# Neighbourhood attention: each head's probabilities divided on GpSimd before they are transposed

## The chip, the cores and the metric

The kernel runs on one core of a Trainium2 chip. The metric is the device time of one execution in microseconds, median of several runs. The core has a matrix engine (TensorE, PE in rows), VectorE (DVE), ScalarE (ACT), GpSimd (POOL) and SyncE (SP), which here only issues DMAs. Each engine works through its own instructions in program order, so an instruction that waits holds up everything behind it on that engine.

## What is computed

One step of a two-layer backbone over 128 context tokens and 2048 latent tokens (a grid of 32 rows by 64 columns), model width 1024. In a layer an input projection feeds four mixers of width 256 each, their gated outputs are joined and go through an output projection and a layer normalisation. The change touches mixer B, the neighbourhood attention of the latent tokens, with 4 heads of 64:

```
s_loc = einsum(q, k of 8 rows x 16 columns around the query) * scale + bias
s_ctx = einsum(q, 256 context keys) * scale
p     = softmax(concat(s_loc, s_ctx))
o     = p_loc @ v_loc + p_ctx @ v_ctx
mixed = o * SiLU(gate)
```

## The kernel before

The time of a layer falls into four stages: input projection and convolution (`phase1`), grouped-query attention (`phase2`), neighbourhood attention (`phase3`), output projection with layer normalisation (`phase4`). The program is written in plain order and a scheduler at build time sets the order on every engine from its own estimate of times; on the chip that order is fixed. It orders TensorE freely in `phase3`.

`phase3` works on 16 tiles of a layer: 8 groups of four grid rows (`NAT_ORDER` = 1, 2, 0, 3, 4, 5, 7, 6), each in a left and a right half (e = 0, 1), so 128 queries a tile. A tile has four heads. Here the heads of a layer are counted through from 0 to 63 in the order of work: head 8 is the first of the third tile. A pair is two heads that share one call of `values`. Inner tiles have 440 local keys and 256 context keys (696 columns); the four tiles of groups 0 and 7 (heads 16 to 23 and 48 to 55, called edge tiles) have 576 columns. For each head:

- S (`scores`, L1222 and L1223): four matmuls into one of two `ps_d` banks.
- TTR (L1228, VectorE): adds the bias, writes `p` to SBUF and takes the row maximum; then m (L1231) negates it. `p` comes from a pool of three buffers (`b3`).
- E (L1232, ScalarE): exp in place, with the row sum into `z`.
- T (`transp`, L1255): five or six transpositions by matmul with the identity, in two parts; VectorE copies part 0 to SBUF (C, L1257), ScalarE part 1 (C', L1259).
- V (`values`, L1270): for a pair of heads, 24 (edge tiles 20) records of values times transposed probabilities into `ps_a`.

`finish` (L1275) ends a tile: reciprocal of the four sums (L1278), copy to a 128x256 tile `zb` (L1279), two matmuls with the identity that spread the reciprocals into the other half of the `ps_a` bank (Z, L1281), and four VectorE products with the gate (L1290): first gate by reciprocal, then by the sums of values.

Two things beside that run in the stage. `load_p4pre` (called at step 8) prepares the output projection's weights: four loads `wo` through two buffers, each cast by ScalarE (woh, L1409) and then subtracted by GpSimd (wol, L1410); the third load needs the buffer that the first wol frees. And `prompt_attn` does the context tokens' attention twice (L1361 to L1391). The first blocks of `phase4` (L1452: `mx`, `mhi`, `mlo`) are prepared late in the stage, and its matmuls (L1492 to L1494) begin while the last heads are still at work.

Of the kernel before, what the change touches and what calls it, by code (L numbers as in the profile page):

```python
# [8 lines left out]
F32 = mybir.dt.float32  # L9
F32R = mybir.dt.float32r  # L10
AF = mybir.ActivationFunctionType
ALU = mybir.AluOpType
# [108 lines left out]
class Kern:  # L121
# [1047 lines left out]
    def _phase3(self, l):  # L1169
        nc, A, S = self.nc, self.A, self.S  # L1170
# [20 lines left out]
        def begin(i, e):  # L1191
            x = tiles.index((i, e))
            if e == 0:
                x = x // 2
                if x + 2 < NT:
                    self.load_nq(NAT_ORDER[x + 2])
                gates[i] = self.b2.tile([128, 2, 256], F32, tag="gt", name="gt")
                c0 = NPR + i * 256
                nc.sync.dma_start(gates[i], S["gate"][256:512, c0:c0 + 256].rearrange("(c p) t -> p c t", p=128))
            d = {"bias": held["tile", i] if d_edge(i) else bi, "v": self.nv[e]}  # L1200
            d["q"] = [
                t[:, :, e * 128:(e + 1) * 128] for t in self.nq[i]
            ]
            d["z"] = self.b2.tile([128, 4], F32, tag="z", name="z")
            st[i, e] = d

        def d_edge(i):
# [2 lines left out]
        def scores(i, e, h):  # L1210
            d = st[i, e]
            k0, nr = self.rows_of(i)
            q = d["q"]
            s = self.bank("d", (128, 1024))
# [3 lines left out]
            n = nr * KC  # L1218
# [5 lines left out]
            p = self.b3.tile([128, NLOC + PAST], F32, tag="p", name="p")  # L1224
            m = self.b3.tile([128, 2], F32, tag="m", name="m")
            n = nr * KC + PAST
# [2 lines left out]
                p[:, :n], s[:, o:o + n], d["bias"][:, h, b0:b0 + n], 1.0, -3.0e38, ALU.add, ALU.max, m[:, 0:1]  # L1229
            )  # L1230
            nc.vector.tensor_scalar(m[:, 1:2], m[:, 0:1], -1.0, None, op0=ALU.mult)  # L1231
            nc.scalar.activation(p[:, :n], p[:, :n], AF.Exp, bias=m[:, 1:2], accum_out=d["z"][:, h:h + 1])  # L1232
            d["p", h] = p

        def chunks(i, e):
# [26 lines left out]
        def values(i, e, pr):  # L1262
            d = st[i, e]
            if pr == 0:
                d["acc"] = self.bank("a", (128, 4, 128))
            ch = chunks(i, e)
            for c, (_, vt, ti) in enumerate(ch):
                for hh in range(2):
                    h = pr * 2 + hh
                    nc.tensor.matmul(  # L1270
                        d["acc"][hh * 64:(hh + 1) * 64, pr, :], vt[:, ti, h * 64:(h + 1) * 64], d["pT", h][:, c, :],
                        start=(c == 0), stop=(c == len(ch) - 1),
                    )

        def finish(i, e):  # L1275
            d = st.pop((i, e))
            zb = self.b2.tile([128, 4, 64], F32, tag="zb", name="zb", bufs=1)
            nc.vector.reciprocal(d["z"], d["z"])  # L1278
            nc.vector.tensor_copy(zb, d["z"].unsqueeze(2).to_broadcast([128, 4, 64]))  # L1279
            for c in range(2):  # L1280
                nc.tensor.matmul(  # L1281
                    d["acc"][:, 2 + c, :], zb[:, 2 * c:2 * c + 2, :].rearrange("p h d -> p (h d)"), self.id,
                    start=True, stop=True,
                )
            gt = gates[i]
            acc = d["acc"].rearrange("p a (r c) -> p a r c", r=4)
            for x in (1, 0):
                for c in range(2):
                    g = gt[:, c, :].rearrange("p (r s c) -> p r s c", r=4, s=2)[:, :, e, :]
                    nc.vector.tensor_tensor(g, acc[:, 2 * x + c], g, op=ALU.mult)  # L1290
            if e == 1:
                c0 = NPR + i * 256
                nc.sync.dma_start(S["mix"][256:512, c0:c0 + 256].rearrange("(c p) t -> p c t", p=128), gates.pop(i))

        pairs = [(i, e, pr) for i, e in tiles for pr in range(2)]
        n = len(pairs)
# [394 lines left out]
```

## Time and profile before

| | us |
|---|---|
| median of 3 runs | 2995.2 |
| lowest and highest of them | 2991.32, 3001.62 |
| the profiled execution's own time | 2991.36 |
| its span, first to last instruction | 2989.6 |
| TensorE busy in the span | 2783.8 (93%) |
| VectorE busy | 2070.4 (69%) |
| GpSimd busy | 1456.9 (49%) |
| ScalarE busy | 1272.3 (43%) |
| `phase3` of layer 0, first S to the first output-projection matmul | 1156.0 to 1315.8 |
| the same in layer 1 | 2630.1 to 2787.4 |

Busy shares of the whole span mix stages with different limits; what counts for this change is what stands in the two stretches of the last two lines. A busy TensorE need not be at its peak, since matmuls overlap in the records.

### The profile page before, as it was taken

How to read it: one execution, taken by the hardware profiler on the slowest of the kernel's cores; microseconds unless marked ns; L12 is line 12 of the kernel's file. 1: busy time of each engine (PE TensorE's matmuls, PEld its weight loads, DVE VectorE, ACT ScalarE, POOL GpSimd, SP SyncE). 2: the span in 40 equal slices, each digit the busy share in tenths (PEclk: the TensorE clock that was granted, in tenths of full speed). 3: DMA queues.
4: the chain of work that ended last, by engine and by line, in shares of the span. 5: the costliest groups of instructions: out<-in, count | busy, mean ns of one | idle time of the engine just before them, and what ended most of it. 6: DMA issues, size and time to landing. Idle time of an engine off the chain costs nothing.

```text
span 2989.6 us, 47085 instructions
## 1 busy us (share of the span) xinstructions
PE 2783.8 (93%) x16944; PEld 2287.9 (77%) x16944; DVE 2070.4 (69%) x4119; ACT 1272.3 (43%) x2376; POOL 1456.9 (49%) x1170
## 2 busy tenths in 40 slices
PE   8888999899899999999989889988899999999998
PEld 6778988889755555887778889988896555578887
DVE  2595168974588886759855971699655788777587
ACT  4454433554344445542224544435533444465311
POOL 4666344654366666004325674456634666740232
PEclk9999999999999999999999999999999999999999
DMA  8343464454370104646642335523443610057342
GB/s 267 106 135 117 131 192 139 127 159 123 102 168 20 34 18 132 158 149 223 212 147 82 116 105 128 160 89 116 146 123 82 144 34 20 24 168 191 132 165 106
DMA packets 390569, 372.82 MB, mean 125 GB/s; under 512 B 52672, under 2 KB 370112, under 8 KB 388800
## 3 DMA queue, kind: packets, MB, share of 16 engines
q1 hardware_dynamic: 390336, 369.82, 42.5%
q8 instruction: 133, 2.18, 0.3%
q14 instruction: 100, 0.82, 0.1%
HBM read 254.66 MB, written 115.06 MB: 124 GB/s over the span
## 4 chain that ended last, share of the span: by engine, by line
PE 56%; DVE 23%; DMA 9%; POOL 4%; ACT 3%; issue 3%; SPq 2%; DVEq 0%; ACTq 0%; POOLq 0%
DVE cacc L755 8%; PE ps_a L1011 7%; PE ps_u L304 5%; PE ps_u L305 5%; PE ps_u L306 5%; PE ps_d L990 4%; PE ps_d L1000 4%; PE ps_d L1493 3%; PE ps_d L1492 3%; PE ps_d L1494 3%; PE ps_a L1270 3%; PE ps_s L928 3%; POOL cac L753 2%; PE ps_s L1255 1%; PE ps_z L928 1%
## 5 line engine op out<-in xcount | busy, mean ns | idle before, releaser
L304 PE MATMUL ps_u<-hhi,whi 128*128 128x384 f32 (+1 forms) x1728 | 576.2, 336 | 2.7 <-ACT hhi L387 2.7
L305 PE MATMUL ps_u<-hlo,whi 128*128 128x384 f32 (+1 forms) x1728 | 576.3, 334 | 1.3 <-DVE hlo L389 0.8
L306 PE MATMUL ps_u<-hhi,wlo 128*128 128x384 f32 (+1 forms) x1728 | 575.3, 333 | 0.0
L1023 POOL TENSOR_TENSOR zp<-zp,e 128x1024 f32<-128x1024 f32 x160 | 385.9, 2412 | 209.8 <-ACT e L1005 206.4
L1005 ACT ACTIVATE e<-ps_d 128x1024 f32<-128x1024 f32 x288 | 292.1, 1024 | 358.6 <-PE ps_d L1000 349.3
L755 DVE SCALAR_TENSOR_TENSOR cacc<-cz,small,cacc 128x208 f32<-128x208 f32 (+2 forms) x840 | 427.5, 565 | 0.3
L419 POOL TENSOR_TENSOR wlo<-ws,whi 128x512 fp32r<-128x512 f32 x188 | 261.1, 1401 | 198.8 <-ACT whi L418 182.8
L304 PEld LDWEIGHTS ps_u<-hhi,whi 128*128 128x128 f32 x1728 | 331.7, 193 | 10.8 <-ACT hhi L387 5.6
L305 PEld LDWEIGHTS ps_u<-hlo,whi 128*128 128x128 f32 x1728 | 332.5, 192 | 6.4 <-POOL hlo L389 2.4
L306 PEld LDWEIGHTS ps_u<-hhi,wlo 128*128 128x128 f32 x1728 | 332.1, 192 | 0.9
L1463 POOL TENSOR_TENSOR mlo<-mx,mhi 128x512 fp32r<-128x512 f32 x66 | 110.4, 1691 | 421.0 <-ACT mhi L1459 405.7
L931 DVE TENSOR_REDUCE mx<-ps_s 128x1 f32<-128x512 f32 (+1 forms) x374 | 228.5, 631 | 107.2 <-PE ps_s L928 102.6
L753 POOL TENSOR_TENSOR cac<-cac,ctm 128x208 f32<-128x208 f32 (+2 forms) x320 | 244.9, 765 | 104.8 <-ACT ctm L752 69.6
L1011 PE MATMUL ps_a<-e,gvv 128*64 128x512 f32 x1152 | 278.2, 604 | 0.0
L304 PE MATMUL ps_u<-whi,hhi 128*128 128x256 f32 x816 | 237.1, 291 | 4.0 <-ACT ev L543 4.0
L306 PE MATMUL ps_u<-whi,hlo 128*128 128x256 f32 x816 | 235.5, 289 | 0.0
L305 PE MATMUL ps_u<-wlo,hhi 128*128 128x256 f32 x816 | 235.5, 289 | 0.0
L752 ACT ACTIVATE ctm<-cz,small 128x208 f32<-128x208 f32 (+2 forms) x320 | 148.5, 472 | 149.7 <-POOL cac L753 91.7
L1493 PE MATMUL ps_d<-wol,mhi 128*128 128x512 f32 x512 | 201.0, 393 | 0.0
L1492 PE MATMUL ps_d<-woh,mhi 128*128 128x512 f32 x512 | 201.0, 393 | 0.0
L1494 PE MATMUL ps_d<-woh,mlo 128*128 128x512 f32 x512 | 200.1, 391 | 0.0
L1000 PE MATMUL ps_d<-q,k 65*128 65x512 f32 x576 | 185.6, 403 | 12.0 <-DMA k<-s_k 12.0
(269 smaller groups left out, 5834.0 us busy)
## 6 DMA issues: line engine op xcount, KB each, us to landing
ws<-in_w_in SPq DMA_DIRECT2D x160, 256.0 KB
mw<-in_w_mod SPq DMA_DIRECT2D x32, 512.0 KB
nq<-s_nq SPq DMA_DIRECT2D x64, 256.0 KB
mx<-s_mix SPq DMA_DIRECT2D x16, 1024.0 KB
s_gate<-ev SPq DMA_DIRECT2D x80, 192.0 KB
s_qh<-qT SPq DMA_DIRECT2D x34, 256.0 KB
x<-in_x SPq DMA_DIRECT2D x17, 512.0 KB
s_xT<-xo SPq DMA_DIRECT2D x17, 512.0 KB
```

Of the source, the lines that this page charges most:

```text
L304: mm(p, ah, bh, start=(k == 0), stop=False)
L305: mm(p, ah, bl, start=False, stop=False)
L306: return mm(p, al, bh, start=False, stop=(k == 7))
L753: nc.gpsimd.tensor_tensor(ac2[:, :n], ac2[:, :n], tm[:, :n], op=ALU.add)
L755: nc.vector.scalar_tensor_tensor(acc[:, c, :n], z[:, c, k:k + n], cw[:, c, k:k + 1], acc[:, c, :n], op0=ALU.mult, op1=ALU.add)
L1000: nc.tensor.matmul(s[:, kv * 512:(kv + 1) * 512], k2[kv][0:65, j * 128:(j + 1) * 128], q2[0:65, 2 * kv:2 * kv + 2, :].rearrange("p h t -> ...
L1005: nc.scalar.activation(e, s, AF.Exp)
L1011: nc.tensor.matmul(acc[kv * 64:(kv + 1) * 64, :], vv[:, j, kv * 64:(kv + 1) * 64], e[:, kv * 512:(kv + 1) * 512], start=(j == 0), stop=(j ...
L1023: nc.gpsimd.tensor_tensor(zp, zp, e, op=ALU.add)
L1492: nc.tensor.matmul(o, hi[:, k, :], woh[:, k, ns], start=(k == 0), stop=False)
L1493: nc.tensor.matmul(o, hi[:, k, :], wol[:, k, ns], start=False, stop=False)
L1494: nc.tensor.matmul(o, lo[:, k, :], woh[:, k, ns], start=False, stop=(k == 7))
```

## The change

Each head's sum now goes into the first column of its own `m`; VectorE takes its reciprocal (R, new L1232), GpSimd multiplies the head's probabilities by it in place (sc, new L1233, 128x696 or 128x576 f32), and the transpositions read the product. The tile `z`, the reciprocal and copy of `finish`, the two Z matmuls and two of the four gate products of a tile go. Lines behind L1204 shift by a few.

```diff
-            d["z"] = self.b2.tile([128, 4], F32, tag="z", name="z")
...
             nc.vector.tensor_scalar(m[:, 1:2], m[:, 0:1], -1.0, None, op0=ALU.mult)
-            nc.scalar.activation(p[:, :n], p[:, :n], AF.Exp, bias=m[:, 1:2], accum_out=d["z"][:, h:h + 1])
+            nc.scalar.activation(p[:, :n], p[:, :n], AF.Exp, bias=m[:, 1:2], accum_out=m[:, 0:1])
+            nc.vector.reciprocal(m[:, 0:1], m[:, 0:1])
+            nc.gpsimd.tensor_scalar(p[:, :n], p[:, :n], m[:, 0:1], None, op0=ALU.mult)
             d["p", h] = p
...
-                d["acc"] = self.bank("a", (128, 4, 128))
+                d["acc"] = self.bank("a", (128, 2, 128))
...
-            zb = self.b2.tile([128, 4, 64], F32, tag="zb", name="zb", bufs=1)
-            nc.vector.reciprocal(d["z"], d["z"])
-            nc.vector.tensor_copy(zb, d["z"].unsqueeze(2).to_broadcast([128, 4, 64]))
-            for c in range(2):
-                nc.tensor.matmul(
-                    d["acc"][:, 2 + c, :], zb[:, 2 * c:2 * c + 2, :].rearrange("p h d -> p (h d)"), self.id,
-                    start=True, stop=True,
-                )
             gt = gates[i]
             acc = d["acc"].rearrange("p a (r c) -> p a r c", r=4)
-            for x in (1, 0):
-                for c in range(2):
-                    g = gt[:, c, :].rearrange("p (r s c) -> p r s c", r=4, s=2)[:, :, e, :]
-                    nc.vector.tensor_tensor(g, acc[:, 2 * x + c], g, op=ALU.mult)
+            for c in range(2):
+                g = gt[:, c, :].rearrange("p (r s c) -> p r s c", r=4, s=2)[:, :, e, :]
+                nc.vector.tensor_tensor(g, acc[:, c], g, op=ALU.mult)
```

The scheduler sets the whole stage anew. On GpSimd, at the start of layer 0's stage, the order of the change is this (L1233 is sc, L1402 is wol, L1079 belongs to the stage before; before, GpSimd had only L1079 and the four wol here):

```order
382 L1233 TENSOR_SCALAR p<-p,m 128x696 [waits DVE_49]
383 L1079 TENSOR_TENSOR accs<-accs,zd 128x512 [waits DVE_49,Activation_49,Pool_49]
384 L1233 TENSOR_SCALAR p<-p,m 128x696 [waits DVE_49] x2
385 L1233 TENSOR_SCALAR p<-p,m 128x696 [waits DVE_49,PE_49] x2
386 L1402 TENSOR_TENSOR wol<-wo,woh 128x2048 [waits DMAHW5_49,Activation_49]
387 L1402 TENSOR_TENSOR wol<-wo,woh 128x2048 [waits DMAHW6_49,Activation_49]
388 L1233 TENSOR_SCALAR p<-p,m 128x696 [waits DVE_49,PE_49] x3
389 L1402 TENSOR_TENSOR wol<-wo,woh 128x2048 [waits DMAHW6_49,Activation_49]
390 L1402 TENSOR_TENSOR wol<-wo,woh 128x2048 [waits DMAHW7_49,Activation_49]
391 L1233 TENSOR_SCALAR p<-p,m 128x696 [waits DVE_49,PE_49] x8
```

So the products of heads 0 to 4 stand ahead of the first two wol, those of heads 5 to 7 between the two pairs, and head 8 behind the last; in layer 1 the order is the same.

On TensorE in the middle of the stage, this is the order of the change from the transpositions of head 34 on (L1256 is T, L1271 V, L1221 and L1222 S; the S is that of head 39, the V that of heads 34 and 35):

```order
5675 L1256 MATMUL ps_s<-small,p 128x128 [waits PE_49,Pool_49]
5676 L1256 MATMUL ps_s<-small,p 128x128 x2
5677 L1256 MATMUL ps_z<-small,p 128x128 [waits PE_49]
5678 L1256 MATMUL ps_z<-small,p 128x128 x2
5679 L1271 MATMUL ps_a<-pT,nv_9314 64x128 [waits DVE_49]
5680 L1256 MATMUL ps_s<-small,p 128x128 [waits PE_49,Pool_49]
5681 L1256 MATMUL ps_s<-small,p 128x128 x2
5682 L1256 MATMUL ps_s<-small,p 128x128 [waits PE_49]
5683 L1256 MATMUL ps_s<-small,p 128x128 x2
5684 L1221 MATMUL ps_d<-ck_9311,nq_12470 128x256 [waits DVE_49]
```

And this is the order of before from the transpositions of head 34 on (L1255 is T, L1270 V; this V is that of the pair before, heads 32 and 33):

```order
5653 L1255 MATMUL ps_s<-small,p 128x128 [waits Activation_49]
5654 L1255 MATMUL ps_s<-small,p 128x128 x2
5655 L1255 MATMUL ps_z<-small,p 128x128 [waits DVE_49]
5656 L1255 MATMUL ps_z<-small,p 128x128 x2
5657 L1270 MATMUL ps_a<-pT,nv_9314 64x128 [waits DMAHW1_49,DMAHW0_49,DMAHW2_49,DVE_49,PE_49]
5658 L1270 MATMUL ps_a<-pT,nv_9314 64x128 x6
5659 L1255 MATMUL ps_s<-small,p 128x128 [waits Activation_49]
5660 L1255 MATMUL ps_s<-small,p 128x128 x2
5661 L1270 MATMUL ps_a<-pT,nv_9314 64x128
5662 L1270 MATMUL ps_a<-pT,cvt 64x128 x4
```

Before, the V behind a pair's first T belongs to the pair before it; after, it is the pair's own V, one T behind. On VectorE this is the order of the change from the TTR of head 37 on (L1227 is TTR with its read of the maximum, L1230 m, L1232 R, L1258 C; the first C is that of head 35, the last that of head 36):

```order
1340 L1227 ISA p,m<-ps_d,bi 128x696 [waits PE_49,Pool_49]
1341 L1227 ISA m 128x1
1342 L1230 TENSOR_SCALAR m<-m 128x1 [waits DVE_49]
1343 L1258 COPY pT<-ps_s 128x384 [waits PE_49]
1344 L1227 ISA p,m<-ps_d,bi 128x696 [waits PE_49,Pool_49]
1345 L1227 ISA m 128x1
1346 L1232 RECIPROCAL m<-m 128x1 [waits Activation_49]
1347 L1230 TENSOR_SCALAR m<-m 128x1 [waits DVE_49]
1348 L1282 TENSOR_TENSOR gt<-ps_a,gt 128x4x32 [waits DMAHW3_49,DMAHW2_49,PE_49]
1349 L1282 TENSOR_TENSOR gt<-ps_a,gt 128x4x32
1350 L1232 RECIPROCAL m<-m 128x1 [waits Activation_49]
1351 L1258 COPY pT<-ps_z 128x384 [waits PE_49]
```

The copy of head 34 stands right ahead of the first of these rows, so the TTR of head 37 follows it; the same holds for head 36 and the TTR of head 39. The R of a pair's first head waits for the exp of the m just ahead of it. On ScalarE the order in a pair is E of head 36, C' of 34, E of 37, C' of 35, E of 38 and so on.

## Rows read from the trace of the kernel before

**Rows 1.** Windows: us, busy of PE, PEld, DVE, ACT, POOL, granted clock, DMA share, GB/s.

```profile
1157.00:1316.00 159.00, 152.25 (x1378) 127.85 (x1376) 118.04 (x360) 95.78 (x210) 24.67 (x9) 0.98 0.69 190
2631.00:2787.00 156.00, 150.60 (x1377) 125.18 (x1377) 116.98 (x359) 95.33 (x210) 25.21 (x9) 0.99 0.70 194
...
1276.00:1296.00 20.00, 17.69 (x157) 15.29 (x157) 12.28 (x42) 10.89 (x26) 1.28 (x1) 0.91 0.78 206
```

**Rows 2.** Groups by line, 1157 to 1316: shapes, count, busy, mean ns, idle before.

```profile
L1290 DVE TENSOR_TENSOR gt<-ps_a,gt 128x128 f32<-128x128 f32 x56 | 13.2, 282 | 1.4 <-PE ps_a L1281 1.0
...
L1281 PE MATMUL ps_a<-small,zb 128*128 128x128 f32 x56 | 10.2, 299 | 0.0
...
L1279 DVE COPY zb<-z 128x256 f32<-128x256 f32 x15 | 7.1, 474 | 0.0
...
L1371 ACT ACTIVATE pp<-ps_d,pm 128x128 f32<-128x128 f32 x8 | 2.8, 361 | 0.8 <-DVE pm L1367 0.8
...
L1278 DVE RECIPROCAL z<-z 128x4 f32<-128x4 f32 x15 | 2.6, 171 | 1.5 <-ACT p L1232 1.5
```

**Rows 3.** Groups by line and form on GpSimd, whole span.

```profile
L1410 POOL TENSOR_TENSOR wol<-wo,woh 128x2048 fp32r<-128x2048 f32 x8 | 36.7, 4609 | 25.9 <-ACT woh L1409 25.9
...
L1124 POOL MEMSET nv<- 128x1024 f32 x4 | 3.7, 958 | 0.0
```

**Rows 4.** Timeline of GpSimd, both layers: start, us, what, idle before.

```profile
1176.91 9.18 POOL L1410 TENSOR_TENSOR wol<-wo,woh 128x2048 fp32r<-128x2048 f32 x2 [8.80 <-ACT woh L1409]
1190.78 9.14 POOL L1410 TENSOR_TENSOR wol<-wo,woh 128x2048 fp32r<-128x2048 f32 x2 [4.70 <-ACT woh L1409]
...
2649.59 9.18 POOL L1410 TENSOR_TENSOR wol<-wo,woh 128x2048 fp32r<-128x2048 f32 x2 [8.49 <-ACT woh L1409]
2662.66 9.16 POOL L1410 TENSOR_TENSOR wol<-wo,woh 128x2048 fp32r<-128x2048 f32 x2 [3.88 <-ACT woh L1409]
```

**Rows 5.** Timeline of TensorE: T of head 8 (both layers), S, T and V.

```profile
1179.44 0.37 PE L1222 MATMUL ps_d<-nk,nq 128*128 128x440 f32 x1
...
1180.08 0.82 PE L1255 MATMUL ps_s<-small,p 128*128 128x128 f32 x6
...
1184.89 0.49 PE L1255 MATMUL ps_s<-small,p 128*128 128x128 f32 x3
...
1192.79 1.09 PE L1270 MATMUL ps_a<-pT,nv 128*64 128x128 f32 x16
...
1194.15 0.38 PE L1270 MATMUL ps_a<-pT,nv 128*64 128x128 f32 x2
...
2657.73 0.49 PE L1255 MATMUL ps_s<-small,p 128*128 128x128 f32 x3
```

**Rows 6.** Timeline of VectorE: a TTR, the C of head 8, a zb copy.

```profile
1160.35 0.87 DVE L1228 CUSTOM_DVE_ANT_0 p<-ps_d,bi 128x696 f32<-128x696 f32 x1
...
1185.49 0.56 DVE L1257 COPY pT<-ps_s 128x384 f32<-128x384 f32 x1 [0.61 <-PE ps_s L1255]
...
1192.66 2.84 DVE L1279 COPY zb<-z 128x256 f32<-128x256 f32 x1
```

**Rows 7.** Timeline of ScalarE: the E behind that TTR, another E, and its C'.

```profile
1161.45 0.88 ACT L1232 ACTIVATE p<-p,m 128x696 f32<-128x696 f32 x1 [2.91 <-DVE m L1231]
...
1170.23 0.86 ACT L1232 ACTIVATE p<-p,m 128x696 f32<-128x696 f32 x1
...
1171.09 0.47 ACT L1259 ACTIVATE pT<-ps_z 128x384 f32<-128x384 f32 x1
```

**Rows 8.** One line's instructions: the output projection's, first and last start, each layer.

```profile
L1492 PE MATMUL ps_d<-woh,mhi x256: 387/389/692, 1315.8 to 1521.2; 128*128 128x512 f32 x128
...
L1492 PE MATMUL ps_d<-woh,mhi x256: 387/389/476, 2787.4 to 2969.3; 128*128 128x512 f32 x128
```

**Rows 9.** Windows at layer 0's start of the stage, columns as in rows 1.

```profile
1164.00:1168.00 4.00, 1.79 (x13) 1.23 (x12) 4.00 (x12) 1.78 (x4) 1.17 (x1) 1.00 0.52 177
1168.00:1172.00 4.00, 4.00 (x30) 3.61 (x31) 3.16 (x11) 2.66 (x8) 0.10 (x1) 0.61 0.54 140
```

## The prediction

> **What bounds the kernel now.** The change lies wholly in `phase3`, so I read first the windows of that stage in both layers [rows 1]: TensorE is busy 152.25 of 159 us in layer 0 and 150.60 of 156 in layer 1, VectorE 118 and 117, ScalarE 96 and 95, GpSimd only 25. TensorE is the engine that ends last, GpSimd has room. Taken by shares, the change moves work from the full engine to the empty one. Then I read the groups by line for what goes [rows 2], the timelines around the four wol for what GpSimd does at the start of the stage [rows 4], and the single instructions of one head for the lengths of a chain [rows 5 to 7]. The reader should see in rows 4 that GpSimd's 25 us are not spread over the stage: they are four long subtractions, from 1176.91 to 1186.09 and from 1190.78 to 1199.92, and the same in layer 1. The new products go into that queue.
>
> **What is removed.** The Z matmuls were busy 10.2 us in 14 tiles of layer 0 [rows 2], 0.7 a tile, some 23 us in all 32 tiles if nothing else ended last. VectorE loses two gate products of 282 ns a tile, a zb copy (mean 474 ns) and one reciprocal (171 ns) [rows 2]. One of these copies took 2.84 us while wol was running [rows 6]; that goes too. VectorE gains a reciprocal and its wait for each head. The nearest row is the 171 ns of the 128x4 one [rows 2]; for 128x1 it can hardly be more and not be below nothing. It lies in a queue that is not the longest (below), so I charge no term.
>
> **What is added on GpSimd.** No row shows a multiply by a column. Above stands a subtraction with two inputs: wol takes 4609 ns for 2048 columns [rows 3], 2.25 ns a column, 1.57 us for 696. Below stands a fill with no input: 958 ns for 1024 [rows 3], 0.94 a column, 0.65 us. One tile input lies between; I take 1.0 us and keep 0.65 and 1.6. At 1.6 us a head GpSimd would still need only 3.2 us for a pair, so it is not the bound by its busy time.
>
> The Trainium skill (GPSIMD Engine Reference, 4.1 Engine selection) holds one-input elementwise work to be roughly at line rate and two-input work about twice slower than on VectorE. By that the multiply would sit near my lower end and take some 0.4 us off each layer; no run here shows it yet.
>
> **First term: the late start of head 8.** The four wol can't move forward. Each waits for a cast, each cast for a load, and the third load for the buffer that the first wol frees, so I take their times from before [rows 4]. The new order puts the products of heads 5 to 7 behind the second wol and that of head 8 behind the fourth. Head 8 is transposed no earlier than 1199.9 + 1.0 (product) + 0.1 (handover) = 1201.0. Before, its T began at 1184.89 [rows 5]: 16.1 us late. In layer 1, 2671.8 + 1.1 = 2672.9 against 2657.73 [rows 4, 5]: 15.2 us late. TensorE can't fill this with other heads, since `p` has three buffers and each is held until its own T. What it can do meanwhile is one V (below).
>
> **Second term: the pace after that.** Before, T of head 8 to the first output-projection matmul took 1315.8 - 1184.89 = 130.9 us, and 2787.4 - 2657.73 = 129.7 in layer 1 [rows 5, 8], prompts and stalls included. After, TensorE's work for an inner pair is two S of 0.64 (1179.44 to 1180.08), twelve T at 0.75 per six, 24 V in 1.36 (1192.79 to 1194.15) [rows 5]: 4.1 us. But the new order puts V right behind its own T, and so one chain goes once round per pair: half of V (0.68), S (0.64), T part 0 to the start of its C (1184.89 to 1185.49, 0.60), C 0.56 [rows 5, 6], then on VectorE the next TTR to its E (1160.35 to 1161.45, 1.10) [rows 6, 7], E to the C' behind it (1170.23 to 1171.09, 0.86), C' 0.47 [rows 7], handover 0.1, and the second half of V again. Sum 5.0 us. VectorE's own chain round a pair (two TTR, two C, one exposed E) is two TTR of 0.9, two C of 0.5 to 0.56, an E of 1.05 with m and R around it, some 4.4 us, and stays below. The multiply is not in the 5.0: each T reads a product begun a good third of a pair earlier or more. For edge tiles I scale by columns, 5.0 x 576/696 = 4.15, an estimate. From T of head 8 to the first output matmul stand 18 inner and 8 edge pairs: 90 + 33 = 123. The prompt blocks sit in the same queues with eight exps of 361 ns and their reads [rows 2]: 5. The wait for the first mix block cost TensorE 2.3 us idle and 9% of clock in 20 us [rows 1]: 4, and stays. One V of 1.4 was done during the late start, and the first pair behind it has looser order: -2. Sum 130. So this term is -0.9 in layer 0 and +0.3 in layer 1: the Z matmuls and the old stalls pay for the chain.
>
> **Third term: the end.** The first output matmul now stands behind V of heads 58 and 59; before, that V (1.4 us) and two tiles' Z (1.4) came behind it, and part of one T (0.35) before it. -2.4 us a layer.
>
> **Fourth term: the clock.** When TensorE was busy 1.79 of 4 us, the next 4 us stood at a granted clock of 0.61, a mix of its two levels of 1.2 and 2.4 GHz [rows 9]; that cost about 1.6 us. The late start leaves TensorE as idle, so I add 1.5 a layer.
>
> Layer 0: 16.1 - 0.9 - 2.4 + 1.5 = 14.3. Layer 1: 15.2 + 0.3 - 2.4 + 1.5 = 14.6. Together 29 us on the profiled execution's 2991.4: 3020. That execution lies 3.8 below the median of the runs shown, so a median may stand up to 4 higher; I say 3021.
>
> **The rivals.** First, *no change*: the late start comes as above, but the chain doesn't bind, because handovers overlap, and the pairs behind head 8 go at TensorE's work, 4.1 inner and 3.8 edge. Then the second term is 18 x 4.1 + 8 x 3.8 + 5 + 4 - 2 = 111, 19 below; with 15.7 late, -2.4 and +1.5 a layer ends 4 us earlier: 2983; with three quarters of that gain it ends level, 2992. For it speaks that before TensorE ran without a gap through most of the stage; against it the order, which leaves no other matmul between T and its V.
>
> Second, *faster*: the products are hidden and all of Z comes back, 2991 - 23 = 2968. It takes that head 8 is not late, so that wol ends 15 us sooner or the pairs make it up and more. Rows 4 speak against it: GpSimd waits there for casts and loads, which this change doesn't touch.
>
> Third, *much slower*: VectorE and GpSimd hinder each other. The zb copy of 2.84 us, six times its mean, ran inside the second stretch of wol [rows 4, 6]. If each C waited so for a product of 1.0 us, half of it on the chain, 26 pairs would lose 1 us each, 52 in both layers: 3073. Against it: the C at 1185.49 took 0.56 us inside the first stretch of wol [rows 4, 6]. C reads PSUM, zb's copy read SBUF.
>
> The Trainium skill (SBUF — State Buffer, Who interferes with whom) has this as a rule: a VectorE copy in a two-port mode and a GpSimd instruction lock each other out for a whole instruction, a VectorE instruction with at most one SBUF input outside those modes does not. Both rows agree with it; by it the remaining TTR, C and gate products would run freely, and the third rival falls.
>
> **How the numbers follow.** Forecast 0.70: 3021. With the multiply at its ends, the chain 0.2 us off per pair (5 us a layer) and the clock between 0 and 3 us a layer its own range is 3005 to 3040. Rival one 0.12 (2983 to 3000), rival two 0.05, rival three or a chain slowed further by low clock 0.13 (3040 to 3075). About 0.3% (9 us) is what a measurement here can tell from no change, so 2986 to 3004 is the same. Slower takes the forecast but 0.02, and rival three: 0.81. Same takes that 0.02 and 0.08 of rival one: 0.10. Faster: 0.09. A range from 2996 to 3048 leaves out about 2 in 10.
>
> **What would show it.** In the new profile: products of some 0.65 to 1.6 us on GpSimd, with gaps of more than 9 us between those of heads 4 and 5 and of heads 7 and 8, filled by wol at nearly the old times; T of head 8 about 15 us later than before, counted from the start of the stage; TensorE busy some 80 to 85% in the inner tiles instead of 100%, waiting for C and C' ahead of V; inner tiles of about 10 us. Both stages of `phase3` some 15 us longer, everything else unchanged. I am wrong if wol moves forward, if the inner tiles take under 9 us, if the multiply takes over 2 us, or if C and TTR grow while products run.

## The result and the profile after

The changed kernel takes 3073.05 us (median of four runs, 3069.22 to 3079.01); the kernel before, on the same chip, 2994.89. The ratio is 1.0255, its 95% interval 1.0234 to 1.0277: slower by 70 to 83 us, where 26 were forecast and 3048 was the end of the range. The sign was right and the size was not. The profiled execution has a span of 3067.1 us, against 2989.6 before.

Where the time went is read from both stages of `phase3`, first their windows (columns as in [rows 1]), then the instructions of two lines in each layer, the score matmuls' and the output projection's first ones (count, ns, first and last start).

```profile
1163.00:1359.00 196.00, 166.00 (x1344) 130.06 (x1344) 114.51 (x363) 98.18 (x211) 145.55 (x72) 0.93 0.56 154
2673.00:2865.00 192.00, 164.02 (x1346) 127.30 (x1344) 114.83 (x363) 98.41 (x211) 144.89 (x72) 0.96 0.58 158
```

```profile
L1221 PE MATMUL ps_d<-nk,nq x64: 305/402/737, 1162.9 to 1356.0; 128*128 128x440 f32 x48, 128*128 128x320 f32 x16
...
L1221 PE MATMUL ps_d<-nk,nq x64: 305/392/737, 2673.3 to 2863.1; 128*128 128x440 f32 x48, 128*128 128x320 f32 x16
```

```profile
L1484 PE MATMUL ps_d<-woh,mhi x256: 388/389/775, 1359.1 to 1564.7; 128*128 128x512 f32 x128
...
L1484 PE MATMUL ps_d<-woh,mhi x256: 387/389/504, 2865.1 to 3046.9; 128*128 128x512 f32 x128
```

From the first score matmul to the first output matmul the stage takes 1359.1 - 1162.9 = 196.2 us in layer 0 and 2865.1 - 2673.3, 191.7 unrounded, in layer 1; before, these were 159.9 and 157.2 (score matmuls from 1156.0 and 2630.1, output matmuls as in [rows 8]). That is +36.3 and +34.5. TensorE is idle for 30 and 28 us of it. The other 6.9 us lie ahead of layer 0's stage, where both kernels issue the same instructions; the later runs, of the old order and the new, put the stage's start anywhere from 1158 to 1173, so this is a spread between executions. Behind the stages nothing changed: from layer 0's first output matmul to layer 1's first score matmul 1314 us in both, and 202 us to the end in both.

GpSimd's groups by form, over the whole span, and its timeline at the start of layer 0's stage (start, us, what, idle time before), to hold against [rows 3, 4]:

```profile
L1233 POOL TENSOR_SCALAR p<-p,m 128x696 f32<-128x696 f32 x96 | 193.7, 2027 | 64.4 <-DVE m L1232 36.8 <-DVE m L1230 24.9 <-PE ps_z L1256 1.4
L1233 POOL TENSOR_SCALAR p<-p,m 128x576 f32<-128x576 f32 x32 | 55.1, 1726 | 23.7 <-DVE m L1232 9.8 <-DVE m L1230 9.3 <-PE ps_s L1256 3.5
```

```profile
1180.19 2.02 POOL L1233 TENSOR_SCALAR p<-p,m 128x696 f32<-128x696 f32 x1 [0.24 <-DVE m L1232]
1182.61 9.06 POOL L1402 TENSOR_TENSOR wol<-wo,woh 128x2048 fp32r<-128x2048 f32 x2 [0.39 <-ACT woh L1401]
1191.65 6.02 POOL L1233 TENSOR_SCALAR p<-p,m 128x696 f32<-128x696 f32 x3
1199.83 9.02 POOL L1402 TENSOR_TENSOR wol<-wo,woh 128x2048 fp32r<-128x2048 f32 x2 [2.16 <-ACT woh L1401]
1208.82 8.03 POOL L1233 TENSOR_SCALAR p<-p,m 128x696 f32<-128x696 f32 x4
```

The product takes 2.03 us, outside the bounds of 0.65 and 1.6. The order is the predicted one: five products, two wol, three products, two wol, and head 8 last. Its T comes at once behind its product; TensorE's timeline in both layers:

```profile
1210.90 0.55 PE L1256 MATMUL ps_s<-small,p 128*128 128x128 f32 x3 [0.39 <-POOL p L1233]
...
2720.62 0.87 PE L1256 MATMUL ps_s<-small,p 128*128 128x128 f32 x6 [1.23 <-POOL p L1233]
```

Counted from the stage's first score matmul, T of head 8 stands at 48.0 and 47.3 us, before at 28.9 and 27.6 [rows 5]: 19.1 and 19.7 us late. From there to the first output matmul it is 148.2 and 144.4 us, before 130.9 and 129.6: another 17.2 and 14.8. These are the two parts of the loss. Of TensorE's idle time some 13 and 12 us lie ahead of this T and 17 and 16 us behind it.

Some of the later orders put head 8 ahead of the last wol, so that the wait falls on a later head. For a cut that holds in all of them I take the TTR of head 16, the first with 576 columns; in every order of the table below that has products it comes behind the last wol. VectorE's timelines in layer 0, of the kernel before, of the changed kernel, and of e1_short and e6_free8 (below):

```profile
1199.39 0.76 DVE L1228 CUSTOM_DVE_ANT_0 p<-ps_d,be 128x576 f32<-128x576 f32 x1 [0.61 <-PE ps_z L1255]
```

```profile
1225.98 0.74 DVE L1227 CUSTOM_DVE_ANT_0 p<-ps_d,be 128x576 f32<-128x576 f32 x1
```

```profile
1228.70 0.74 DVE L1227 CUSTOM_DVE_ANT_0 p<-ps_d,be 128x576 f32<-128x576 f32 x1
```

```profile
1222.52 0.75 DVE L1227 CUSTOM_DVE_ANT_0 p<-ps_d,be 128x576 f32<-128x576 f32 x1
```

How TensorE's time divides, worked out from its timelines: for each group of matmuls the time from its start to the start of the next, without the idle time shown between them, summed over the stage (layer 0 / layer 1, us; prompts, 8 us, left out). The last two columns are the stage up to the TTR of head 16 and from there to the first output matmul; with a fourth buffer a TTR can run a head further ahead, so there they mark a slightly earlier point.

```
kernel                  stage          idle          S + T + V        Z          up to TTR 16   from there
before                  159.9 / 157.2   6.5 /  5.3   137.7 / 137.2   7.2 / 7.0   43.4 / 41.2    116.5 / 116.0
after                   196.2 / 191.7  30.1 / 28.5   158.4 / 155.7   -           63.1 / 60.8    133.1 / 130.9
e1_short                189.1 / 191.1  25.9 / 27.2   155.6 / 155.9   -           60.3 / 59.7    128.8 / 131.4
e2_half                 192.6 / 190.2  27.8 / 28.1   156.6 / 154.2   -           61.7 / 59.3    130.9 / 130.9
e9_wide                 191.7 / 191.9  25.6 / 28.8   158.5 / 155.4   -           59.3 / 57.7    132.4 / 134.2
e6_free8                166.4 / 169.0   9.6 / 11.2   149.1 / 150.0   -           49.5 / 49.8    116.9 / 119.2
e13_tt                  176.9 / 176.5  15.0 / 16.7   153.7 / 152.1   -           55.0 / 55.1    121.9 / 121.4
e14_p4                  181.7 / 186.5  21.6 / 21.9   151.0 / 155.2   -           58.1 / 58.3    123.6 / 128.2
e15_p3ctl               195.7 / 193.2  30.0 / 27.4   157.5 / 157.9   -           64.3 / 61.8    131.4 / 131.4
e16_tt_p4               163.8 / 164.2   9.1 /  7.8   146.5 / 148.7   -           48.5 / 49.5    115.3 / 114.7
e7_none                 159.3 / 164.8   4.2 /  7.0   147.4 / 150.2   -           43.1 / 44.7    116.2 / 120.1
```

Each row is one profiled execution; these lie up to 15 us from the median of their kernel's runs (e9_wide 15 below, e6_free8 12 above), so a few us between two rows say nothing.

So the loss is idle time (23.6 us in layer 0) and dearer S, T and V (20.7), less 7.2 for the Z matmuls. Not all of the 20.7 is another order of groups. The granted clock of the stage was 0.93 and 0.96, before 0.98 and 0.99; busy time times the missing share makes some 9 and 5 us of it (an estimate). And a group with a wait behind it is counted with its whole length, while otherwise the next group starts before it ends: such waits stand behind 53 and 51 groups, before behind 6 and 7. What is left goes with the order: S stands in 62 and 61 runs (before 50 and 52) and V in 66 and 67 (before 52 and 51), T in fewer, 61 (before 82 and 83).

What TensorE does in the idle time behind head 8 is shown by the chain of waits through one inner pair of the changed kernel (start, us, what; L1271 is V, L1221 and L1222 S, L1256 T, L1258 C, L1227 TTR):

```profile
1220.24 1.52 PE ps_a L1271 x22
1221.77 0.34 PE ps_d L1221
...
1222.50 0.34 PE ps_s L1256 x3
1222.84 0.02 issue
1222.86 0.35 DVE pT L1258
1223.21 0.12 issue
1223.34 0.87 DVE p L1227
...
1224.27 0.42 PE ps_d L1221
...
1225.07 0.34 PE ps_z L1256 x3
1225.41 0.02 issue
1225.44 0.57 DVE pT L1258
1226.01 0.04 issue
1226.05 1.52 PE ps_a L1271 x22
```

5.8 us for this pair: nearly the whole V 1.5, S 0.75, T 0.34, C 0.5, TTR with its handover 0.9, S 0.8, T 0.34, C 0.6. TensorE and VectorE take turns. It is one of the longer pairs: from one whole V to the next, inner pairs without a prompt beside them take 4.5 to 6.1 us, most of them 5.1 to 5.2. Of the idle time behind T of head 8, 12.2 and 11.3 us end with a C, 0.7 and 0.4 with a product. No product stands in the chain. The same is seen from the product's side, in the instructions of line L1233 from 1210 to 1330, among "who waited for it (us, times)":

```profile
  PEld ps_s L1256: 0.8, 1
  PEld ps_z L1256: 0.7, 1
  PE ps_z L1256: 0.4, 1
  PE ps_s L1256: 0.4, 1
```

In 120 us and 43 products TensorE waited some 2 us for one. This made the first theory: the order costs the time, and the price of the product doesn't.

### The profile page after: what moved, and what is told of

It reads as the page before. It is cut to its first block, busy times and chain, and to the rows that moved or that the text cites. A ratio compares the mean times of both kernels' runs of the same rounds, so it can differ in the third digit from the quotient of the medians.

```text
span 3067.1 us, 47191 instructions
## 1 busy us (share of the span) xinstructions
PE 2813.3 (92%) x16816; PEld 2292.9 (75%) x16816; DVE 2062.0 (67%) x4119; ACT 1277.5 (42%) x2376; POOL 1733.7 (57%) x1298
## 4 chain that ended last, share of the span: by engine, by line
PE 55%; DVE 21%; DMA 8%; POOL 6%; ACT 4%; issue 3%; SPq 2%; DVEq 0%; ACTq 0%; POOLq 0%
PE ps_a L1011 7%; DVE cacc L755 7%; PE ps_u L304 5%; PE ps_u L306 5%; PE ps_u L305 5%; PE ps_d L990 4%; PE ps_d L1000 4%; PE ps_d L1484 3%; PE ps_d L1486 3%; PE ps_d L1485 3%; PE ps_s L928 3%; PE ps_a L1271 3%; POOL cac L753 2%; PE ps_z L928 1%; POOL wlo L419 1%
## 5 line engine op out<-in xcount | busy, mean ns | idle before, releaser
L755 DVE SCALAR_TENSOR_TENSOR cacc<-cz,small,cacc 128x208 f32<-128x208 f32 (+2 forms) x840 | 416.0, 551 | 0.3
L419 POOL TENSOR_TENSOR wlo<-ws,whi 128x512 fp32r<-128x512 f32 x188 | 290.6, 1558 | 190.8 <-ACT whi L418 181.6
L304 PEld LDWEIGHTS ps_u<-hhi,whi 128*128 128x128 f32 x1728 | 334.1, 194 | 11.9 <-ACT hhi L387 6.0
L1233 POOL TENSOR_SCALAR p<-p,m 128x696 f32<-128x696 f32 (+1 forms) x128 | 248.6, 1952 | 88.1 <-DVE m L1232 46.6
```

The costliest lines, as they stand in the source:

```text
L304: mm(p, ah, bh, start=(k == 0), stop=False)
L419: nc.gpsimd.tensor_tensor(lo[:, ks, :], w, f32(hi[:, ks, :]), op=ALU.subtract)
L755: nc.vector.scalar_tensor_tensor(acc[:, c, :n], z[:, c, k:k + n], cw[:, c, k:k + 1], acc[:, c, :n], op0=ALU.mult, op1=ALU.add)
```

## The experiments

Ratios are to the kernel before, run on the same chip; intervals of 95%. Theory A says that the order sets the pace; theory B, that the price of the product does.

**e1_short and e2_half**: the order held, the products cut. Once the scheduler has placed every instruction, the operands of the products are narrowed to 8 and to 348 columns:

```
+    todo[k] = i.__replace__(ins=[narrow(x) for x in i.ins], outs=[narrow(x) for x in i.outs])
```

> Every instruction stands in the order of the changed kernel; only the products on GpSimd are cut to 8 columns a head (most probabilities stay undivided), so that each takes some 0.1 to 0.2 us in place of 2.03. Theory A (the order): after wol, TensorE and VectorE take turns on one chain through a whole V, two S, two T with their C and one TTR, 5.8 us an inner pair, and the products lie beside it. Then only the late start shrinks, by the product of head 8 and a little, 2 to 4 us a layer, and some waits near the products: 3055 to 3068. Theory B (the price): the two products of a pair, 4.06 us of its 5.8, are on the chain; without them the pace falls to the forecast 130 us and the late start to 17: 3073 - 2 x 20 = 3033 or less.

> As e1_short, but the products are cut to 348 columns, by 2.9 ns a column 1.0 us each: just the price that the prediction took. If the prediction was wrong only in the price, this runs in the predicted 3021. Theory A: 3060 to 3070, since the products are not on the chain. Theory B: about half of the way, 3050.

Measured: 1.0228 (1.0202 to 1.0254) and 1.0213 (1.0191 to 1.0235). The products took 306 and 1153 ns (GpSimd's groups of e1_short and of e2_half):

```profile
L1233 POOL TENSOR_SCALAR p<-p,m 128x8 f32<-128x8 f32 x128 | 39.0, 306 | 262.6 <-DVE m L1232 142.7 <-DVE m L1230 82.3 <-PE ps_s L1256 21.2
```

```profile
L1233 POOL TENSOR_SCALAR p<-p,m 128x348 f32<-128x348 f32 x128 | 147.2, 1153 | 171.8 <-DVE m L1232 89.2 <-DVE m L1230 59.0 <-PE ps_s L1256 11.5
```

In this order, cheap and nearly free products win 8 to 13 us of 78; the two intervals overlap, so which of the two wins more is not shown. In e1_short T of head 8 stands at 45.7 and 46.7 us, and the rest takes 143.5 and 144.4; in e2_half these are 47.1 and 46.3, and 145.5 and 143.9. Theory B, as it stood, falls.

**e3_vector, e4_scalar, e8_parity**: the product on other engines, the order free.

```
-            nc.gpsimd.tensor_scalar(p[:, :n], p[:, :n], m[:, 0:1], None, op0=ALU.mult)
+            nc.vector.tensor_scalar(p[:, :n], p[:, :n], m[:, 0:1], None, op0=ALU.mult)     # e3, and even heads of e8
+            nc.scalar.activation(p[:, :n], p[:, :n], AF.Copy, scale=m[:, 0:1])             # e4, and odd heads of e8
```

> The product on VectorE in place of GpSimd, the order free. The late start by wol is gone (16 us a layer or more). VectorE's round for an inner pair is two TTR, m and R of 1.2, two C of 0.56 and two products. At 1.0 us a product (the rate of C, 1.46 ns a column) it is 5.7 us, as slow as the changed kernel's pace, and the stage ends some 19 us a layer earlier by the late start alone: 3030 to 3040. At 0.4 us it is 4.4 us, near TensorE's own work, and the Z matmuls' gain shows: 2960 to 2990.

> The product on ScalarE (a copy with the column as scale) in place of GpSimd, the order free. It can hardly cost less than E of the same tile, 0.88 us. ScalarE's pair is then two E of 0.97, two products of 0.88 and two C' of 0.47, 4.6 us, above TensorE's 4.4 by the rows of the changed kernel; the late start by wol is gone, the cast woh is on this engine too. Theory A: the time depends on the chain of the new order, 5 us a pair: 2990 to 3015. If ScalarE's load alone decides, 18 x 4.6 + 8 x 3.9 is 114 a layer and it is 2975 to 2990.

> The product of each even head on VectorE (0.77 us by the run with all products there), of each odd head on ScalarE (0.87), the order free. A pair then loads VectorE with two TTR, m and R of 1.25, two C of 0.56, one product and the gates, 4.6 us, and ScalarE with two E of 0.97, two C' of 0.47 and one product, 3.8 us; both are near TensorE's 4.4. Neither wol nor a full engine stands in the way, so if load and the late start were all, 2970 to 2990; if the longer way from E to T costs pace whatever engine takes the product, 3000 to 3020, as with all products on ScalarE.

Measured: 1.0109 (1.0087 to 1.0131), 1.0051 (1.0031 to 1.0071) and 1.0104 (1.0071 to 1.0136). On VectorE the 696 columns took 765 ns, on ScalarE 869. Taking the work off GpSimd gives back between a good half and four fifths of the loss; e4_scalar's 3010 (1.0051 of 2994.89) is the number of theory A. Sharing it out between two engines, which by load should have been best, is no better than VectorE alone, so the load of an engine does not decide. By 2994.89, e8_parity's 3026 lies above both of its numbers, the second (3000 to 3020) being the nearer, and e3_vector's 3028 lies between its two, near the one for a dearer product than it had.

**e5_first3**: only heads 0 to 11 off GpSimd, onto ScalarE.

> The products of the first three tiles (heads 0 to 11) are made on ScalarE (a copy with the column as scale, 0.87 us by the run with all products there), those of all later heads on GpSimd as in the changed kernel. So GpSimd has wol and no product beside it at the start of the stage. If the late start is wol's, T of head 8 comes back to some 30 us behind the first score matmul (47 to 48 in the changed kernel) and the rest keeps its slow pace: 3073 - 2 x 17 = 3039, between 3030 and 3048. If the late start comes from the longer chain of each head, it stays: 3060 or more.

Measured: 1.0164 (1.0134 to 1.0194), 27 us less than the changed kernel's 1.0255, where 34 were expected. T of head 8 stands at 31.2 and 36.4 us again, and the rest takes 149.6 and 149.0. So the products behind wol cost about that; the slow pace stays.

**e6_free8 and e7_none**: the order made anew for a product of 8 columns, and for none.

```
-            nc.gpsimd.tensor_scalar(p[:, :n], p[:, :n], m[:, 0:1], None, op0=ALU.mult)
+            p8 = p[:, :n].rearrange("p (a b) -> p a b", a=8)[:, :, 0]                      # e6 alone
+            nc.gpsimd.tensor_scalar(p8, p8, m[:, 0:1], None, op0=ALU.mult)                 # e6 alone
```

> The source multiplies 8 columns of a head, 87 (72) apart, so that each transposition still waits for its product, and the instructions are ordered anew, as the scheduler places them for a product that it takes for short. Instructions and costs are those of the run with 8 columns in the changed kernel's order (3071); only the order differs. Theory A (the order sets the pace): T of head 8 to the first output matmul falls from 144 us to 125 to 132, a late start by wol stays: 3010 to 3035. If the order does not matter and the chain of a head through four engines does, it stays at 3055 to 3071. Most probabilities stay undivided.

> The line of the product is taken out (the probabilities stay undivided), everything else of the change stays, the order is free. It shows the most that the removal of the spread sums can give: the Z matmuls' 0.7 us a tile, 23 us in all, and a less busy VectorE: 2960 to 2975. If TensorE had not been the bound before, 2985 to 3000.

Measured: 1.0048 (1.0029 to 1.0068) and 0.9995 (0.9979 to 1.0012). e6_free8 has the instructions and nearly the costs of e1_short, which stood at 1.0228; only the order differs, and its stages are 22.7 and 22.1 us shorter: 10.8 and 9.9 us of it up to the TTR of head 16, 11.9 and 12.2 from there. The total is at the lower end of theory A's range, but not by its division: the late start, which was to stay, shrinks too, since the new order puts products between the wol and head 8 ahead of the last two. With e7_none the first number missed: with no product at all, the removal of the spread sums wins nothing. The time is the second number's, but not for its reason, since TensorE is idle for 4.2 and 7.0 us only. In the table its Z is gone (7 us), but S, T and V cost 9.7 and 13.0 us more than before. They stand in more and smaller groups (V in 69 and 74 groups, before 52 and 51), and a small group is dear, as two lines of TensorE's timeline of e7_none show:

```profile
1226.29 0.43 PE L1270 MATMUL ps_a<-pT,nv 128*64 128x128 f32 x2
1226.65 0.39 PE L1221 MATMUL ps_d<-ck,nq 128*128 128x256 f32 x1
...
1227.93 0.66 PE L1270 MATMUL ps_a<-pT,nv 128*64 128x128 f32 x8
1228.52 0.44 PE L1255 MATMUL ps_s<-small,p 128*128 128x128 f32 x2
```

Two V matmuls hold TensorE for 0.36 us until the next group starts, eight for 0.59.

**e9_wide and e11_wide_scalar**: the reverse of e1_short. The order is made for 8 columns, then the products are widened to all columns, on GpSimd and on ScalarE.

> The whole change with full products on GpSimd, but every instruction in the order of e6_free8, which the scheduler made for products of 8 columns (the products are widened to all columns once the order stands). Nothing is left out. If the order alone sets the pace (theory A pure), it runs near e6_free8, 1.005 to 1.012 of the kernel before. If price and order set it together, the short order has no room for two products of 2.03 us a pair and TensorE waits for them in place of the chain: 1.018 to 1.03, as slow as the changed kernel.

> As e9_wide, with the product on ScalarE (0.87 us): the order is planned for products of 8 columns, then they are widened to all. Nothing is left out. The run with all products on ScalarE and its own order stood at 1.005. If the order planned for a short product is the better one, 0.998 to 1.003; if the planned room for the product is needed, 1.008 or more.

Measured: 1.0205 (1.0163 to 1.0247) and 1.0041 (1.0020 to 1.0061). On GpSimd theory A in its pure form falls: the good order is lost once the products have their length. The wait now shows at the product (line L1234 of e9_wide from 1210 to 1330, who waited for it):

```profile
  PEld ps_s L1257: 10.5, 16
  PEld ps_z L1257: 7.0, 10
  PE ps_s L1257: 6.9, 10
  PE ps_z L1257: 4.6, 6
```

On ScalarE, where the product is 0.87 us, the foreign order costs nothing against the product's own one (1.0051); the measured ratio lies between the two that were expected. So a product of 2.03 us is paid once, either in the order that makes room for it or in waits for it; a new theory, C: it is the length of the way from E to T, held against the three buffers of `p`. A buffer is taken by a TTR and free again when T has read it; the longer the way between, the less far ahead of T the TTR of a later head can stand.

**e10_zcut**: the kernel before in its order, the Z matmuls narrowed like the products of e1_short.

> The kernel before in its own order; only the Z matmuls stream 8 columns in place of 128 (the gate products of the spread sums read one of these columns, so the attention's output is not normalised rightly). It shows what TensorE gets back when the Z matmuls go and nothing else moves. By the time from the start of one group of matmuls to the start of the next, Z is 7.2 us a layer: 14 us, 2980 to 2985, 0.995 of the kernel before. By the sum of the prediction's rows (0.7 us a tile) 23 us: 0.992. If TensorE is not the bound, 1.000.

Measured: 0.9983 (0.9967 to 0.9999), 5 us. By the starts of the groups the Z matmuls still hold TensorE for 6.3 and 6.1 us with 8 columns, so this run doesn't price them. By the table they hold TensorE for 7.2 and 7.0 us, so that some 14 us, not 23, are the most that their removal alone could give (an estimate); no run takes them out in the old order.

**e12_forms**: GpSimd alone.

> The changed kernel with 18 extra instructions on GpSimd at its very start, three of each form on 128x696 f32: the product by a column in place and into another tile, the product by a constant, the product of a tile and a spread column as a two-input operation, the difference of two tiles, a copy. If one-input work has the rate of one input, the first three and the copy take 0.65 to 1.0 us and the two-input ones 1.57 (2.25 ns a column); if the product by a column is slow as such, 2.03 in both places, and the constant and the copy tell what the column costs.

GpSimd's groups by form, first 200 us:

```profile
L1548 POOL TENSOR_SCALAR fb<-fa,fr 128x696 f32<-128x696 f32 x3 | 6.1, 2027 | 0.3
L1547 POOL TENSOR_SCALAR fa<-fa,fr 128x696 f32<-128x696 f32 x3 | 6.1, 2023 | 0.3
L1549 POOL TENSOR_SCALAR fb<-fa 128x696 f32<-128x696 f32 x3 | 5.8, 1948 | 0.2
L1551 POOL TENSOR_TENSOR fb<-fa,fb 128x696 f32<-128x696 f32 x3 | 4.9, 1649 | 0.2
L1550 POOL TENSOR_TENSOR fb<-fa,fr 128x696 f32<-128x696 f32 x3 | 4.0, 1345 | 0.2
L1552 POOL COPY fb<-fa 128x696 f32<-128x696 f32 x3 | 2.3, 762 | 0.1
```

In place or not, by a column or a constant, the product as tensor-by-scalar takes 1.95 to 2.03 us; the same product as a two-input operation with the spread column takes 1.35, less than the difference of two tiles (1.65). The copy takes 0.76.

**e13_tt, e14_p4, e15_p3ctl, e16_tt_p4**: the cheaper form, a fourth buffer for `p`, the control of the memory moves that this needs, and form and buffer together.

```
-            nc.gpsimd.tensor_scalar(p[:, :n], p[:, :n], m[:, 0:1], None, op0=ALU.mult)
+            nc.gpsimd.tensor_tensor(p[:, :n], p[:, :n], m[:, 0:1].to_broadcast([128, n]), op=ALU.mult)   # e13, e16
...
-            p = self.b3.tile([128, NLOC + PAST], F32, tag="p", name="p")
+            p = self.b3.tile([128, NLOC + PAST], F32, tag="p", name="p", bufs=4)                         # e14, e16
```

> The product on GpSimd as a two-input operation of the tile and the spread column: 1.35 us by the run of the forms, in place of 2.03; order free. The prediction's price range was 0.65 to 1.6, so this is the change at a price that the prediction had in view. If the price was its fault, about 3025 to 3035 (1.010 to 1.013). If the way from E to the transposition costs by its length with three buffers of p, in step with the product: between 1.005 (product 0.3) and 1.0255 (2.03), so 1.014 to 1.022.

> The changed kernel with four buffers for p in place of three; the room comes from one gate buffer in place of two and from a prompt tile that moves into another. Full products of 2.03 us on GpSimd. If the three buffers make the pace, T of head 8 to the first output matmul falls from 144 to 148 to about 130, and TensorE can also do one head more before wol: 1.008 to 1.015. If the order or the engines' turns make it whatever the buffers, 1.022 to 1.028.

> The changed kernel with the same moves in memory as e14_p4, but three buffers of p. Control: 1.023 to 1.028 like the changed kernel; anything else is the price or the gain of one gate buffer.

> The product of 1.35 us as in e13_tt and four buffers of p as in e14_p4. If length and buffers are the cause, both gains add: the pace is near TensorE's own work and only wol's late start of 8 to 15 us a layer is left: 1.002 to 1.010. If not, it stands with the worse of the two.

Measured: 1.0097 (1.0072 to 1.0121), 1.0141 (1.0109 to 1.0174), 1.0241 (1.0218 to 1.0263) and 1.0028 (1.0007 to 1.0050). The control stands with the changed kernel. A third off the product's length gives back three fifths of the loss, a fourth buffer some two fifths, both together nearly all: idle time falls from 30 to 9 us, and from the TTR of head 16 on e16_tt_p4 is as fast as the kernel before. That length and buffers both count is what theory C says. Its sizes were not right: e13_tt came out below the 1.014 to 1.022 that it gave, where the price alone had put it or a little below, and in e14_p4 the time from T of head 8 on is 141.1 and 147.7 us, not about 130. Nor does length alone rank the versions: on VectorE a product of 0.77 us stood at 1.0109, on GpSimd one of 1.35 us at 1.0097.

**e17_first3_tt_p4 and e18_scalar_p4**: does any version with divided probabilities beat the kernel before?

> As e16_tt_p4 (1.003: two-input product of 1.35 us on GpSimd, four buffers of p), with the products of heads 0 to 11 on ScalarE, so that wol stands before no product that TensorE needs soon. In e16_tt_p4 T of head 8 stood 1.5 to 4 us later than before; this comes back: 0.999 to 1.002. If the split of the groups on TensorE holds what is left, no change against 1.003.

> All products on ScalarE (0.87 us) with four buffers of p; with three it stood at 1.005. If the buffers were what held it, 0.997 to 1.002; if ScalarE's own load of 4.6 us a pair is the limit, 1.003 to 1.006.

Measured: 1.0020 (1.0006 to 1.0034) and 1.0061 (1.0039 to 1.0083). None does. The fourth buffer does nothing for ScalarE's version.

## Why the prediction was wrong, point by point

**The bound.** TensorE was the full engine, but what Z gave back was not 23 us. In the table Z holds TensorE for 7 us a layer, and e7_none shows that a new order eats even these. So the Z matmuls could not pay for the chain, as the second term had it.

**The product.** Taken at 1.0 us between 0.65 and 1.6, measured at 2.03. Both bounds were rows of GpSimd, and both missed the form: a fill and a two-input operation don't enclose the tensor-by-scalar one. With a product inside the bounds (e13_tt) the ratio is 1.0097, by 2994.89 a time of 3024, inside the range. The price didn't act as a term of its own, though: e13_tt's stages are 19.3 and 15.2 us shorter than the changed kernel's, while the same order with products of 1.15 us (e2_half) is 3.6 and 1.5 us shorter. The price works through the order that is made for it. A product over 2 us was also one of the prediction's own signs of being wrong.

The Trainium skill (GPSIMD Engine Reference, 4.1 Engine selection) calls one-input work roughly line rate. The copy at 0.76 us, as long as VectorE's product of the same columns (0.77), bears it out; the one-input product at 2.03 does not, and here the measurement decides.

**First term, the late start.** The mechanism was right: wol stood where it was said, and T of head 8 came behind it. 19.1 and 19.7 us stand against 16.1 and 15.2. 1.0 us of the gap is the product's price; the rest is that the second pair of wol ended 2.0 and 3.5 us later, counted from the stage's start, than was taken from before.

**Second term, the pace: this is the step that failed.** Forecast -0.9 and +0.3 us, 130 us from T of head 8 to the first output matmul; measured 148.2 and 144.4, that is +17.2 and +14.8. The product's price is not what failed it: in the very order that the prediction read, products of 1.15 us (e2_half) left 145.5 and 143.9 us and a ratio of 1.0213, by 2994.89 some 3059, beyond the range.

That one chain goes round once a pair, with TensorE waiting for a copy between T and V, was right. Its sizes were too small. In layer 0, from one whole V to the next, a plain inner pair took 5.3 us on average where 5.0 were forecast, and an edge pair 4.9 where 4.15 were scaled from the inner one by its columns; the prompts added some 7.5 us, not 5, and the wait for the first mix block some 6, not 4. That is 16 of the 18 us that layer 0 took longer than forecast; the rest lies at the first and the last pair. The way round was another, too: forecast through half a V, one S, T, C, E and C', measured, in the pair shown, through a whole V, two S, two T, two C and a TTR. And S, T and V were charged at their old spacing, 4.1 us a pair, so that TensorE was to be busy 80 to 85% in the inner tiles; it was busy some 90%.

And "the multiply is not in the 5.0" was true of the chain and wrong of the cause: the scheduler had spread the order out to make room for the product, so that its length was paid without a wait for it (e1_short, e6_free8, e9_wide). The prediction took the new order as given and asked only what each instruction costs in it.

The reciprocal, for which no term was charged, does wait: VectorE was idle 18.2 us ahead of R, for E, in the 145 us from 1205 to 1350 (its line stands with the rivals below). e7_none keeps R in that queue (8.4 us idle ahead of it from 1205 to 1330) and takes the time of the kernel before, so this wait alone is not the loss.

How length and buffers share the 17 us between them is not settled: a fourth buffer or a cheaper product shortens the stage, but every such run has an order of its own. Against the control (131.4 us in both layers from the TTR of head 16 on) the fourth buffer alone gives 7.8 and 3.2 us there; against the changed kernel the cheaper product alone gives 11.2 and 9.5, and both together 17.8 and 16.2.

**Third term, the end.** Forecast -2.4 us a layer, measured nothing (1314 and 202 us in both kernels).

**Fourth term, the clock.** Taken at 1.5 us a layer. The windows of the late start:

```profile
1176.00:1196.00 20.00, 14.81 (x102) 11.91 (x104) 7.97 (x24) 9.10 (x14) 19.37 (x8) 0.76 0.88 240
1196.00:1216.00 20.00, 14.88 (x96) 11.42 (x94) 7.63 (x26) 9.72 (x16) 17.84 (x7) 0.77 0.27 93
1216.00:1236.00 20.00, 18.15 (x176) 14.81 (x172) 12.37 (x44) 10.60 (x24) 14.10 (x8) 1.00 0.44 107
```

While TensorE waited around wol its granted clock was 0.76, a mix of 1.2 and 2.4 GHz, for 40 us. At full clock its 29.7 us there would be some 23 (an estimate from 0.76), so up to 7 us; how much of it lay under the wait for wol and cost nothing is not known. Over the whole stage the estimate above is some 9 and 5 us, where 1.5 were taken.

**The rivals.** "No change" and "faster" fell. "Much slower" named 3073, and that is the time, but by luck: VectorE is not held up by GpSimd. (The same chance also covered a chain slowed further by a low clock, which is nearer to what came.) VectorE's groups from 1205 to 1350, while GpSimd was making products most of the time (compare [rows 6]):

```profile
L1227 DVE CUSTOM_DVE_ANT_0 p<-ps_d,bi 128x696 f32<-128x696 f32 x34 | 29.7, 874 | 0.2
...
L1258 DVE COPY pT<-ps_s 128x384 f32<-128x384 f32 x21 | 11.7, 556 | 10.0 <-PE ps_s L1256 9.8
L1232 DVE RECIPROCAL m<-m 128x1 f32<-128x1 f32 x50 | 8.0, 160 | 18.2 <-ACT p L1231 18.0
```

TTR 874 and C 556 ns, as before. The Trainium skill's rule (SBUF — State Buffer, Who interferes with whom), by which this rival was to fall, is borne out: C has its input in PSUM, TTR one of its two in PSUM.

## What to carry to other kernels

Where a scheduler places the instructions, a longer way between two steps is paid in the order even when no engine ever waits for it in the trace; so ask how many buffers the way goes through, and test with the order held and the cost cut, and the reverse. The share of a full engine that an operation's busy time claims is no gain in store: count the time from its start to the next group's, and look whether a new order cuts the remaining work into smaller, dearer groups, as in e7_none. Before an elementwise operation goes to GpSimd, price its very form there, and look for what else stands in that queue.

## What the runs showed of the hardware

On GpSimd a product by a column costs 0.31, 1.15, 1.73 and 2.03 us for 8, 348, 576 and 696 columns of f32: 2.5 ns a column and 0.28 us at the start. The two-input form of the same product costs 1.35 us, two thirds of it, and the copy 0.76; which form an operation is written in was worth 1.6% of this kernel, with the order made anew for each. The same 696 columns cost 0.77 us on VectorE and 0.87 on ScalarE. On TensorE two matmuls standing alone between other groups held it for 0.36 us, a run of eight for 0.59.
